# Normalised rows: scaled on the vector engine and transposed, in place of float32 products with a diagonal

## The chip, the core and the metric

The kernel runs on one core of a Trainium2 chip. The metric is device time in microseconds, the median of several runs; the profile is that of one execution.

## The reference

One inference step of a two-layer trunk for 384 tokens (128 context tokens, 256 latent tokens) of width 1024. Each layer has a mixer (retention, Hyena convolution and mLSTM side by side) and a ConvFFN. Ahead of either stands a normalisation with modulation, cut here to what matters:

```python
def rmsnorm(x, g):
    xf = x.astype(jnp.float32)
    return xf * lax.rsqrt(jnp.mean(xf * xf, axis=-1, keepdims=True) + EPS) * g

def trunk_layer(x, cvec, lp, init, latent):
    ...
    h = rmsnorm(x, lp['norm_mix_pre']) * (1.0 + sc1) + sh1
    mix, states = mixer(h, lp, init, latent)
    x1 = x + g1 * rmsnorm(mix, lp['norm_mix_post'])
    h = rmsnorm(x1, lp['norm_ffn_pre']) * (1.0 + sc2) + sh2
    out = x1 + g2 * rmsnorm(conv_ffn(h, lp), lp['norm_ffn_post'])
```

So h is needed four times: for the mixer and for the ConvFFN of two layers.

## The kernel before, in words

**Tiles.** The 384 tokens are three blocks t = 0, 1, 2 of 128 rows; block 0 is the context. `x[t]` holds a block with tokens on partitions and 1024 columns. The projections need h the other way round, with 128 channels on partitions and tokens along the row, in eight pieces, and each piece as a high and a low part in the type fp32r (`hh`, `hl`): every large product is made of three (high by high, high by low, low by high). Weights stream in by DMA (`raw`) and are split in the same way: the scalar engine casts the high part (`hi`), the vector engine subtracts it for the low part (`lo`). In the turns some of these pieces lie in a tile named `aside`.

**From x to h.** `norm_pre(t)` (L732) takes the mean square of a block on the scalar engine, in two halves of 512 columns (`junk`); `rms` (L286) adds them on the vector engine (`rs`) and takes the power -1/2 on GpSimd (`rr`, one value for each row). The vector engine then multiplies an identity matrix by these values, row by row: a diagonal `diag` of 128x128 (L740). `norm_P(t, c)` (L748) multiplies four pieces of 128 columns of x by this diagonal on the tensor engine, in float32; with x as the stationary operand this scales the rows and transposes them in one step, into half c of the block in a PSUM bank. `norm_M` (L756) applies scale and shift of the modulation, four 128x128 pieces for each half (`hf`): half 0 on the scalar engine, half 1 on the vector engine, but for block 1 of the second layer's mixer, where both are on the scalar engine. `norm_S` (L769) casts the high part on the scalar engine (`hh`) and subtracts it on the vector engine (`hl`).

**The four places.** (1) The start, before the mixer of the first layer: `norm_pre` for all three blocks beside the filter spectra, `norm_P` for blocks 0 and 1 ahead of the bias and the last two modulation products (`times(6)`, `times(7)`, L436), `norm_P` for block 2 after the modulation is finished (`start`, L416 to L538). (2) and (4), the turn from mixer to ConvFFN in each layer: `w_out` (L1355) finishes the accumulators of a block, `residual` (L1332) squares them on the scalar engine, multiplies them by the gate on the vector engine (`yg`), takes `rs` and `rr` and adds the result to `x`; then `norm_pre(t)`. The transposition of block 0 is queued between the last products of blocks 1 and 2; those of blocks 1 and 2 stand in `first_up` (L1393), around the first products of the ConvFFN. (3) The turn from the first layer to the second: the same behind the last products of the ConvFFN (L1467 to L1477), with blocks 1 and 2 within the first projection of the mixer (`group`, L784, the branch for `"m"` and group 0).

**Order.** The order on the engines' queues is made by a planner that takes, of the instructions that it believes ready, the one of highest priority; `high_priority(offset=300)` puts residuals and norms ahead of the splits of weights. `issue_after` puts an instruction behind a named one of its engine: `norm_T_after` (L776) puts the products with the diagonal behind all that the tensor engine has been given so far. In the start, `self.strict` fixes the order as written, for the tensor engine first and for vector and scalar engine later.

**Buffers.** `diag` has three buffers in the pool `tmp`, which is opened for the start and again at each turn from mixer to ConvFFN, on the space of the closed mixer pool; the pool of the ConvFFN is opened behind it.

Lines in the traces: L208 is `mm`, L212 is `tp`, L255 `tt`, L260 and L262 `ts`, L266 `stt`, L274 `act`, L278 `copy`.

Of the kernel before, what the change touches and what calls it, by code (L numbers as in the profile page):

```python
# [37 lines left out]
# the largest float32 by which half a turn stays within the range of the sine  # L38
# [3 lines left out]
# ---------------------------------------------------------------- host side: layout and shape constants  # L42
# [8 lines left out]
def _constants():  # L51
# [6 lines left out]
    # minus one for each of the three parts of a head's row  # L58
# [10 lines left out]
    # even and odd tokens, the lower half of the frequencies: the upper half is their sum with  # L69
    # the other sign, conjugated  # L70
# [31 lines left out]
def _layout(inp):  # L102
# [8 lines left out]
    # rows of the modulation vectors: block j of 512 columns sits at partitions 32j (context) and 32j + 1 (latent)  # L111
# [14 lines left out]
    def token_major(m):  # L126
        # (L, D, 4*384) -> per group of 384 columns, two chunks of four 128-row blocks
        m = m.reshape(L, 2, 4, 128, 4, 384)
        return m.transpose(0, 4, 1, 3, 2, 5).reshape(L, 8, 128, 1536)
# [3 lines left out]
    # the gates ride along with the first 384 columns  # L133
# [7 lines left out]
    # per-partition columns  # L141
# [11 lines left out]
    # the filter networks of both layers side by side, 64 partitions each  # L153
# [34 lines left out]
# ---------------------------------------------------------------- device side  # L188

class Trunk:  # L190
    # banks of the accumulators of w_out, by block of tokens
# [13 lines left out]
    # -------- small helpers  # L205
# [8 lines left out]
    def in_order(self, engine):  # L214
        """The engines in self.strict take their work as it is written here."""
        last = getattr(self, engine)
        return self.tc.issue_after(last.ins) if engine in self.strict and last else nullcontext()

    def after(self, *last):
        """Behind these on their engines."""  # L220
        stack = ExitStack()
        for i in last:
            stack.enter_context(self.tc.issue_after(i.ins))
        return stack

    # -------- PSUM: eight banks, each a queue of its own
# [3 lines left out]
    def turn(self, s):  # L230
        """The next bank of a set taken in turns."""
        i = self.turns[s]
        self.turns[s] = i + 1
        return self.bank(self.sets[s][i % len(self.sets[s])])
# [51 lines left out]
    def rms(self, s2):  # L286
        """The reciprocal root of the mean square, from the two halves of the mean."""
        t = self.tiny.tile([128, 1], F32, tag="rs1", name=self.nm("rs"), bufs=4)
        self.stt(t, s2[:, 0:1], EPS, s2[:, 1:2], ALU.add, ALU.add)
        r = self.tiny.tile([128, 1], F32, tag="rr", name=self.nm("rr"), bufs=4)  # L290
        self.nc.gpsimd.tensor_tensor(r, t, self.mhalf[:, 0:1], ALU.pow)  # L291
        return r

    def log_sigmoid(self, out, z, P, n):
        """min(z, 0) - log1p(exp(-|z|)), log1p with the rounding of its argument put back."""
        tl = lambda: self.tiny.tile([P, n], F32, tag=f"ls{n}", name=self.nm("ls"), bufs=4)
        a, e, u, l = tl(), tl(), tl(), tl()
        self.ts(a, z, -1.0, ALU.mult)
        self.tt(a, a, z, ALU.min)
        self.act(e, a, AF.Exp)  # L300
        self.ts(u, e, 1.0, ALU.add)
        self.act(l, u, AF.Ln)
        self.stt(u, u, 1.0, e, ALU.subtract, ALU.subtract)
        self.tt(l, l, u, ALU.subtract)
        self.stt(out, z, 0.0, l, ALU.min, ALU.subtract)

    # -------- weights
# [18 lines left out]
    def load_weights(self):  # L326
        """The loads of the next chunk of the stream, in halves."""
# [14 lines left out]
    def splits(self, key, raws):  # L342
        """High and low parts of a chunk, in steps."""
        halves, steps = [], []
        # at the turn of a block the buffers are still taken, but the one of the spectra is idle
# [5 lines left out]
        for raw in raws:  # L351
            m = raw.shape[1]
            hi, lo = new("hi"), new("lo")
            # finer where the vector engine also has the norms between two projections to do
# [22 lines left out]
    # -------- setup  # L377
    def setup(self):
# [21 lines left out]
        # silu of both conditioning vectors, as stationary columns  # L400
# [15 lines left out]
    def start(self, fp):  # L416
        """Modulation and normalised rows of the first projection, and the filter spectra of both
        layers beside them; the loads in the order in which they are needed."""
# [7 lines left out]
        def rows(k):  # L426
            """Modulation weights, in the buffers of the weights as long as these are idle."""
# [44 lines left out]
        def warm(n):  # L472
            """Products of no use that take the tensor engine's clock out of its rest while the first
            loads are on their way."""
# [18 lines left out]
        # the bias  # L493
# [69 lines left out]
    def fill(self, n=1):  # L563
        """Streams the next blocks of modulation weights beside the projections."""
# [11 lines left out]
    def mod(self, l, s):  # L576
        """Superblock s of the modulation of layer l: (sh1 | sc1), (g1 | sh2), (sc2 | g2)."""
# [11 lines left out]
    def mod_beside(self, l, s):  # L589
        """The same with the products on the vector engine, where only that one has time to spare."""  # L590
# [54 lines left out]
    def gate_rows(self, l, g):  # L645
        """A gate times its norm gain, over all partitions: [128, context / latent, D]."""
# [5 lines left out]
    # -------- hyena filter spectra  # L652
    def filter_hidden(self, fp, w1, w2, col, meanwhile):
        """The hidden layers of the filter networks of both layers: [128, tokens] for each layer,
        64 rows of its own and a row of ones."""
# [4 lines left out]
        for i, wt in enumerate((w1, w2)):  # L660
# [5 lines left out]
            # in turns, less the nearest whole number  # L666
# [15 lines left out]
    def filter_taps(self, fp, l, h, w3):  # L682
        """Sum and difference of the forward and the backward filters."""
# [15 lines left out]
    def filter_spectra(self, fp, l, taps):  # L699
        nc = self.nc  # L700
        # spectra [frequency, tile, cos / sin, order, channel]
# [15 lines left out]
    def butterfly(self, s, d, a, b):  # L717
        """s = a + b, d = a - b, of two PSUM tiles."""
# [8 lines left out]
    # -------- normalised, modulated activations, transposed and split  # L727
# [4 lines left out]
    def norm_pre(self, t):  # L732
        """A diagonal of the reciprocal root mean squares of the rows of x."""
# [5 lines left out]
        d = self.tmp.tile([128, 128], F32, tag="diag", name=self.nm("diag"), bufs=3)  # L739
        self.ts(d, self.ident, r, ALU.mult)  # L740
        self.xn[t] = d

    def norm_T(self, t, where, h, psf):
        """Tokens of block t modulated, transposed and split into the tiles of h."""
# [3 lines left out]
    def norm_P(self, t, c, ps):  # L748
        for k in range(4):
            self.mm(ps[:, 128 * k:128 * k + 128], self.x[t][:, 512 * c + 128 * k:512 * c + 128 * k + 128], self.xn[t])  # L750
        return ps
# [24 lines left out]
    def norm_T_after(self, *a):  # L776
        """norm_T behind the products queued so far."""
# [6 lines left out]
    def group(self, key, l, g, between=None):  # L784
        """Token-major columns g of an input projection: three [128, 384] accumulators."""
# [12 lines left out]
        if key == "m" and g == 0:  # L798
            # the first tokens are there before the last ones
# [36 lines left out]
    def heads_T(self, src, tag):  # L836
        """[128 tokens, 4 * 96] -> [96, 4, 128]."""
# [7 lines left out]
    def head_norm(self, src, out):  # L845
        """out = src * 0.5 * rsqrt(mean(src^2) + eps) by head, [128, 4, 96]; src in SBUF."""
# [9 lines left out]
    # -------- gates of the mLSTM  # L856
    def gates(self, l, pss):
# [5 lines left out]
        # [token, direction, tile, head]  # L863
# [6 lines left out]
        # the splits of the next weights let the gates go first  # L870
# [3 lines left out]
    def stabilisers(self, l, g5, lf):  # L874
# [9 lines left out]
        # rows [head, direction, tile, token]  # L884
# [13 lines left out]
        # [head, (previous, last), direction, tile]  # L898
# [21 lines left out]
        # previous and last stabilisers over all partitions: [128, 2, direction, tile, head]  # L920
# [22 lines left out]
    def row_parts(self, mr):  # L943
        """The stabilisers as three bfloat16 parts that add up to them, 32 partitions apart."""
# [13 lines left out]
    # -------- mLSTM  # L958
# [117 lines left out]
    def channel_major(self, outs, ws, hh, hl):  # L1076
        """Two [128 columns, 384 tokens] products from a chunk [rows of k, 2 * 128 columns]."""
# [9 lines left out]
    # -------- Hyena  # L1087
    def long_conv(self, z, o):
        """z: two [128 channels, 384] tiles -> PSUM tiles of the long convolution, the latent rows
        with the even ones first."""  # L1090
# [10 lines left out]
        # spectra: [frequency, cos / sin, channel] of the context, of the latent rows in two halves  # L1101
# [34 lines left out]
    def conv3(self, out, ps, col):  # L1136
        """Three taps along the tokens, context and latent apart; ps [128, 384] in PSUM."""
# [5 lines left out]
    def hyena(self, l, hs):  # L1143
# [30 lines left out]
        # projections beside the long convolutions  # L1174
# [9 lines left out]
    # -------- retention  # L1184
# [46 lines left out]
    def retention(self, l, M, kd, qd, cd):  # L1231
# [75 lines left out]
        # the first rows of w_out while the gates are on their way  # L1307
# [13 lines left out]
    def token_major(self, outs, blocks, first=False, last=False):  # L1321
        """outs: two [128 tokens, 512] accumulators; blocks: (x high, x low, 128 rows of weights [128, 1024])."""
# [8 lines left out]
    # -------- residual with post-norm  # L1331
    def residual(self, t, accs, g):  # L1332
        """x[t] += g * rmsnorm(accs); accs: two PSUM tiles of 512 columns."""
# [42 lines left out]
    # -------- ConvFFN  # L1376
    def ffn(self, l, g):
        nc = self.nc
        with self.tc.tile_pool(name=f"ffn{l}", bufs=2, reuse_waits="tile") as fp:
# [13 lines left out]
            def first_up():  # L1393
                """The first two chunks, beside the norms: in the order in which the operands get there."""
# [4 lines left out]
                # the context first, while the last latent rows are still being normalised  # L1399
# [16 lines left out]
                # into what the first start has cleared of the banks  # L1416
# [80 lines left out]
    def run(self):  # L1497
# [11 lines left out]
        for l in range(DEPTH):  # L1509
            xp_s.close()  # L1510
            with tc.tile_pool(name=f"mx{l}", bufs=1, reuse_waits="tile") as self.mx:
# [6 lines left out]
                # not among the gates, where it would cost loads of function tables  # L1518
# [45 lines left out]
```

## Time and profile before

| | |
|---|---|
| three runs | 1355.83, 1358.76, 1360.96 us |
| median | 1358.76 us |
| span of the profiled execution | 1355.0 us |
| tensor engine busy | 1339.3 us (99%) |
| vector engine busy | 890.6 us (66%) |
| scalar engine busy | 568.8 us (42%) |
| GpSimd busy | 35.3 us (3%) |
| DMA | 217.27 MB, mean 160 GB/s |

The page gives the profiled execution no time of its own beside its span. The span runs from the first to the last instruction. Engines are called PE (tensor engine), PEld (its weight loads), DVE (vector engine), ACT (scalar engine), POOL (GpSimd). A row such as `diag<-c_ident,rr` says what is written and, behind the arrow, what is read; `b` is a PSUM bank. A float32 product appears as two instructions, products of fp32r and transposes as one. Products overlap in the tensor engine: the next one starts before the last has ended, so the step from one start to the next is what it costs the engine, and the time shown for a run of products is from the first start to the last end.

### The profile page before, as it was taken

The page shows a single profiled execution, that of the slowest core. Times are in us where ns is not written, and L with a number is a line of the kernel's source. Part 1 is how long each engine was busy: PE and PEld are TensorE (multiplying, and loading weights), DVE is VectorE, ACT ScalarE, POOL GpSimd, SP SyncE. Part 2 cuts the span into 40 slices and gives each one's busy share as a digit, 9 for nine tenths or more (in the row PEclk, how much of TensorE's full clock was granted, in tenths as well). Part 3 has the DMA queues.
Part 4 walks back from the last instruction along what each step waited for, and adds up shares of the span by engine and source line. Part 5 has one row for each costly group of instructions (what it writes and reads, how often), then busy time and mean ns, then how long its engine had stood idle before and what let it go on. Part 6 is the DMA issues. An engine that isn't in the chain of part 4 may idle for free.

```text
span 1355.0 us, 19419 instructions
## 1 busy us (share of the span) xinstructions
PE 1339.3 (99%) x7527; PEld 1206.1 (89%) x7527; DVE 890.6 (66%) x1594; ACT 568.8 (42%) x944; POOL 35.3 (3%) x64
## 2 busy tenths in 40 slices
PE   8999999999999999999999999999999999999997
PEld 2788788889998998899899999988999999999996
DVE  5657666667887899799557578666645545545445
ACT  3654253464333333333247543546433333333333
POOL 1100000000000000000000000000000000000000
PEclk9999999999999999999999999999999999999999
DMA  9864557344665565665335232424434334333331
GB/s 354 290 249 148 181 168 238 101 164 151 212 227 172 191 237 176 212 221 181 116 112 192 95 95 73 143 92 173 143 118 137 126 117 136 124 121 131 124 122 50
DMA packets 59101, 217.27 MB, mean 160 GB/s; under 512 B 7214, under 2 KB 9456, under 8 KB 53632
## 3 DMA queue, kind: packets, MB, share of 16 engines
q1 hardware_dynamic: 59008, 216.02, 46.7%
q8 instruction: 59, 0.97, 0.3%
q14 instruction: 34, 0.28, 0.1%
HBM read 210.06 MB, written 5.94 MB: 159 GB/s over the span
## 4 chain that ended last, share of the span: by engine, by line
PE 91%; DMA 5%; DVE 2%; ACT 1%; issue 1%; POOL 0%; SPq 0%; DVEq 0%; POOLq 0%; ACTq 0%
PE b L208 90%; DMA mraw<-in_w_mod 1%; DMA raw<-in_w_up 1%; PE b L212 1%; DMA hi<-in_w_mod 1%; DMA lo<-in_w_mod 1%; DMA raw<-in_w_in_m 1%; DVE lo L255 1%; ACT junk L274 0%; ACT hi L278 0%; DMA c_tri<-in_c_tri 0%; DMA w<-in_f_w 0%; DVE mr L908 0%; POOL rr L291 0%; DVE x L266 0%
## 5 line engine op out<-in xcount | busy, mean ns | idle before, releaser
L255 DVE TENSOR_TENSOR lo<-raw,hi 128x1024 fp32r<-128x1024 f32 (+3 forms) x288 | 321.2, 1129 | 216.9 <-ACT hi L278 214.3
L278 ACT CAST hi<-raw 128x1024 fp32r<-128x1024 f32 (+3 forms) x288 | 275.4, 973 | 411.7 <-PE b L208 387.5
L208 PE MATMUL b<-hh,lo 128*128 128x384 f32 (+1 forms) x1120 | 367.9, 336 | 0.0
L208 PE MATMUL b<-hh,hi 128*128 128x384 f32 (+2 forms) x1120 | 364.8, 334 | 0.0
L208 PE MATMUL b<-hl,hi 128*128 128x384 f32 x1088 | 362.5, 338 | 0.0
L208 PEld LDWEIGHTS b<-hh,hi 128*128 128x128 f32 x1120 | 205.7, 188 | 4.6 <-issue 2.5
L208 PEld LDWEIGHTS b<-hh,lo 128*128 128x128 f32 x1120 | 208.0, 188 | 0.1
L208 PEld LDWEIGHTS b<-hl,hi 128*128 128x128 f32 x1088 | 203.7, 188 | 1.2
L208 PE MATMUL b<-lo,hh 128*128 128x384 f32 (+2 forms) x474 | 164.8, 352 | 1.9 <-DVE lo L255 1.9
L208 PE MATMUL b<-hi,hh 128*128 128x384 f32 (+2 forms) x468 | 165.5, 357 | 0.9 <-ACT hh L1347 0.8
L208 PE MATMUL b<-hi,hl 128*128 128x384 f32 (+2 forms) x468 | 162.7, 351 | 0.0
L266 DVE SCALAR_TENSOR_TENSOR cv<-b,pcol,cv 128x127 f32<-128x127 f32 (+1 forms) x256 | 100.6, 414 | 93.9 <-ACT cv L274 89.4
L208 PE MATMUL b<-lo,gh 128*128 128x512 f32 x384 | 151.7, 395 | 0.0
L208 PE MATMUL b<-hi,gh 128*128 128x512 f32 x384 | 150.6, 392 | 0.0
L208 PE MATMUL b<-hi,gl 128*128 128x512 f32 x384 | 150.2, 391 | 0.0
L274 ACT ACTIVATE cv<-b,pcol 128x384 f32<-128x384 f32 x64 | 43.0, 672 | 178.6 <-PE b L208 178.4
L266 DVE SCALAR_TENSOR_TENSOR macc<-mraw,sil,macc 128x512 f32<-128x512 f32 x168 | 113.3, 746 | 0.0
L208 PEld LDWEIGHTS b<-hi,hh 128*128 128x128 f32 x468 | 87.8, 188 | 16.1 <-issue 8.0
L208 PEld LDWEIGHTS b<-lo,hh 128*128 128x128 f32 x474 | 89.1, 188 | 7.3 <-DVE lo L255 3.7
L208 PEld LDWEIGHTS b<-hi,hl 128*128 128x128 f32 x468 | 87.9, 188 | 4.5 <-issue 0.7
L208 PEld LDWEIGHTS b<-hi,gh 128*128 128x128 f32 x384 | 72.1, 188 | 17.5 <-issue 2.5
L208 PEld LDWEIGHTS b<-lo,gh 128*128 128x128 f32 x384 | 72.1, 188 | 17.2 <-issue 3.4
(242 smaller groups left out, 1221.2 us busy)
## 6 DMA issues: line engine op xcount, KB each, us to landing
raw<-in_w_up SPq DMA_DIRECT2D x128, 512.0 KB, 4.6
mraw<-in_w_mod SPq DMA_DIRECT2D x40, 1024.0 KB, 5.1
raw<-in_w_down SPq DMA_DIRECT2D x64, 512.0 KB, 4.3
raw<-in_w_in_r SPq DMA_DIRECT2D x32, 384.0 KB, 3.1
raw<-in_w_in_m SPq DMA_DIRECT2D x24, 384.0 KB, 6.3
raw<-in_w_out SPq DMA_DIRECT2D x16, 512.0 KB, 4.1
raw<-in_w_in_h SPq DMA_DIRECT2D x12, 512.0 KB, 3.7
mraw<-in_w_mod SPq DMA_DIRECT2D x8, 512.0 KB, 10.0
```

The source lines that it names most:

```text
L208: self.pe = self.nc.tensor.matmul(out, lhsT=lhsT, rhs=rhs, start=start, stop=stop, **kw)
L212: self.pe = self.nc.tensor.transpose(out, in_, self.ident[:n, :n])
L255: self.dve = self.nc.vector.tensor_tensor(o, a, b, op)
L266: self.dve = self.nc.vector.scalar_tensor_tensor(o, a, s, b, op0, op1)
L274: self.scalar = self.nc.scalar.activation(o, a, f, **kw)
L278: self.scalar = self.nc.scalar.copy(o, a)
```

## The change

`norm_pre` no longer makes a diagonal. It multiplies the two halves of x by the reciprocal root mean square on the vector engine, into two tiles `xs` of 128x512 float32, six buffers in the same pool. `norm_P` transposes four pieces of such a half by `tp`, the transpose of the tensor engine with the identity, in place of the products of x with the diagonal. Everything else is as before; comments that went are left out here.

```diff
     def norm_pre(self, t):
-        """A diagonal of the reciprocal root mean squares of the rows of x."""
         s2 = self.tiny.tile([128, 2], F32, tag="s2", name=self.nm("s2"), bufs=6)
         for c in range(2):
             jk = self.tmp.tile([128, 512], BF16, tag="junkn", name=self.nm("junk"), bufs=1)
             self.act(jk, self.x[t][:, 512 * c:512 * c + 512], AF.Square, scale=D ** -0.5, accum_out=s2[:, c:c + 1])
         r = self.rms(s2)
-        d = self.tmp.tile([128, 128], F32, tag="diag", name=self.nm("diag"), bufs=3)
-        self.ts(d, self.ident, r, ALU.mult)
-        self.xn[t] = d
+        halves = []
+        for c in range(2):
+            xs = self.tmp.tile([128, 512], F32, tag="xs", name=self.nm("xs"), bufs=6)
+            self.ts(xs, self.x[t][:, 512 * c:512 * c + 512], r, ALU.mult)
+            halves.append(xs)
+        self.xn[t] = halves
...
     def norm_P(self, t, c, ps):
         for k in range(4):
-            self.mm(ps[:, 128 * k:128 * k + 128], self.x[t][:, 512 * c + 128 * k:512 * c + 128 * k + 128], self.xn[t])
+            self.tp(ps[:, 128 * k:128 * k + 128], self.xn[t][c][:, 128 * k:128 * k + 128])
         return ps
```

## Rows read from the trace of the kernel before

**Rows 1.** The page's table of engines: busy time, share of the span, instructions

```profile
PE 1339.3 (99%) x7527; PEld 1206.1 (89%) x7527; DVE 890.6 (66%) x1594; ACT 568.8 (42%) x944; POOL 35.3 (3%) x64
```

**Rows 2.** The chain that ended last, in order of time: start, us, what

```profile
284.78 0.30 DVE diag L260
285.13 155.55 PE b L208 x890
...
708.63 23.93 PE b L208 x140
```

**Rows 3.** Timeline of PE, first turn from mixer to ConvFFN: start, us, instruction

```profile
285.13 2.05 PE L208 MATMUL b<-diag,x 128*128 128x128 f32 x16 [0.16 <-DVE diag L260]
...
292.52 1.95 PE L208 MATMUL b<-diag,x 128*128 128x128 f32 x16
...
298.27 0.61 PE L208 MATMUL b<-hh,lo 128*128 128x128 f32 x4
...
299.61 2.00 PE L208 MATMUL b<-diag,x 128*128 128x128 f32 x16
...
303.18 2.60 PE L208 MATMUL b<-hh,aside 128*128 128x256 f32 x20
```

**Rows 4.** DVE timeline; window: busy PE, PEld, DVE, ACT, POOL, granted clock, DMA

```profile
284.99 1.43 DVE L255 TENSOR_TENSOR yg<-b,G 128x512 f32<-128x512 f32 x2
...
291.22 1.28 DVE L255 TENSOR_TENSOR lo<-raw,aside 128x512 fp32r<-128x512 f32 x2
...
298.93 0.29 DVE L260 TENSOR_SCALAR diag<-c_ident,rr 128x128 f32<-128x128 f32 x1 [0.41 <-POOL rr L291]
...
284.80:299.90 15.10, 14.94 (x108) 13.78 (x108) 12.86 (x29) 12.05 (x30) 2.20 (x4) 1.00 0.27 102
```

**Rows 5.** The same turn: timeline of ACT

```profile
300.75 1.51 ACT L274 ACTIVATE hf<-b,modT,modT 128x128 f32<-128x128 f32 x4 [1.58 <-PE b L208]
302.29 1.37 ACT L278 CAST hh<-hf 128x512 fp32r<-128x512 f32 x2
```

**Rows 6.** Groups by line and form: count | busy us, mean ns | idle before

```profile
L208 PE MATMUL b<-diag,x 128*128 128x128 f32 x192 | 23.8, 278 | 1.1 <-DVE diag L260 1.0 <-ACT hf L274 0.2
...
L260 DVE TENSOR_SCALAR macc<-mraw,sil 128x512 f32<-128x512 f32 x24 | 9.8, 480 | 1.7 <-DMA mraw<-in_w_mod 1.7
...
L212 PE MATMUL b<-c_ident,hs 128*128 128x128 f32 x36 | 5.0, 275 | 0.0
```

**Rows 7.** Timeline of PE in the first mixer: twelve transposes, a product behind them

```profile
82.33 1.47 PE L212 MATMUL b<-c_ident,k 128*96 128x128 f32 x12
...
85.18 0.33 PE L208 MATMUL b<-hi,hl 128*128 128x384 f32 x1
```

**Rows 8.** Timeline of DVE: four scalings of 128x512 in a row

```profile
336.17 1.67 DVE L260 TENSOR_SCALAR macc<-mraw,sil 128x512 f32<-128x512 f32 x4
```

**Rows 9.** Timeline of the start: PE, DVE, ACT

```profile
34.57 3.84 PE L208 MATMUL b<-diag,x 128*128 128x128 f32 x32 [0.35 <-DVE diag L260]
...
44.73 2.05 PE L208 MATMUL b<-diag,x 128*128 128x128 f32 x16 [0.17 <-ACT hf L274]
...
41.20 0.88 DVE L266 SCALAR_TENSOR_TENSOR modbm<-b,c_onecol,modbm 128x256 f32<-128x256 f32 x2 [5.08 <-PE b L208]
...
39.20 1.99 ACT L278 CAST hi<-raw 128x400 fp32r<-128x400 f32 x4 [9.37 <-DMA raw<-in_w_in_q]
```

**Rows 10.** Timeline of DVE and PE in the turn from layer to layer

```profile
721.02 1.05 DVE L255 TENSOR_TENSOR lo<-raw,hi 128x400 fp32r<-128x400 f32 x2
...
721.08 1.50 PE L208 MATMUL b<-lo,hh 128*128 128x400 f32 x6
...
724.23 1.25 PE L208 MATMUL b<-lo,hh 128*128 128x400 f32 x6
```

**Rows 11.** Timeline of PE in the start: float32 products

```profile
4.51 1.65 PE L208 MATMUL b<-feat,w 33*128 33x384 f32 x2
...
26.48 4.56 PE L208 MATMUL b<-w,fh 128*128 128x512 f32 x10
```

## The prediction

> **What bounds the kernel now.** I read the engine table first. The tensor engine is busy for 99% of the span and the vector engine for 66% [rows 1], so over the whole kernel the change trades time of the engine that is full for time of one that is not. That is only an average, so I read next the chain of work in order of time. It shows the four places where rows are normalised: the start, the turn from mixer to ConvFFN in either layer, and the turn from the first layer to the second. At the last three the chain leaves the vector engine's `diag` and stays with the tensor engine from there on: 890 instructions in a row from 285.13, 140 from 708.63 [rows 2] (the turn of the second layer, at 930.22, repeats the first). So no wait ends late behind a diagonal today, and every product with one lies on the path. The timelines of such a turn are the third view. The tensor engine does the diagonal products of block 0 at 285.13, of block 1 at 292.52 and of block 2 at 299.61, with other products packed between [rows 3]. Block 2 is the tight one. Its `diag` is finished at 299.22 [rows 4], the scalar engine waits 1.58 us for the first half of its products and ends the first half of `hh` at about 302.9 (302.29 + half of 1.37) [rows 5], and the first products that need this start at 303.18 [rows 3]. The slack is about 0.25 us.
>
> **The tensor engine's part.** The change takes away eight float32 products of x with a diagonal per block and puts eight transposes there. The trace records 192 instructions for the 96 products, so two for each [rows 6]. What counts is how long the engine starts them: the run of 16 less the last one's own 0.27 us, which is 2.05 - 0.27 = 1.78 us for block 0 and 1.95 - 0.27 = 1.68 for block 1 [rows 3]. Twelve transposes of the same 128 columns take 1.47 us with the last one's own 0.27 in it, which is (1.47 - 0.27) / 11 = 0.109 us each [rows 6, 7]. Eight make 0.87 us. A block is thus 0.91 or 0.81 us shorter, a turn of three blocks 2.5 us.
>
> The Trainium skill (TensorE: Matmul & The Clock Gate, Part 4) has about 275 ns for a transpose within a kernel. Eight of these one after another would be 2.2 us, and a block would get longer by some 0.4 us, the kernel by some 5 us. The trace has the same duration, 275 ns [rows 6], but starts them 0.109 us apart [rows 7], so I use the spacing.
>
> **The vector engine's part.** It loses one 128x128 scaling of 0.29 us per block [rows 4] and gets two of 128x512. The nearest row of this form (scalar from a column, float32, SBUF to SBUF) is the first step of `macc`: 480 ns for one [rows 6], 1.67 us for four in a row, so 0.40 us from start to start [rows 8]. A pair holds the queue for 0.8 us where the diagonal held it for 0.2 (284.78 to 284.99 [rows 2, 4]): 0.6 us more per block, 7 us in all. The first transpose can start 0.48 - 0.29 = 0.2 us later than the first product did. The second half is there 0.40 us after the first, and four transposes take 0.44, so no second wait comes of it. Nothing is added to the GpSimd or DMA queues.
>
> What stands behind the pair is `yg` of the next block, which has to run before that block's root mean square, residual and second norm. So the pair of block 0 delays the route of block 1, and that of block 1 the route of block 2. From 284.8 to 299.9 the vector engine is busy for 12.86 of 15.10 us [rows 4]; what is left are mostly waits for GpSimd's power, which lie on the route itself. The one filler ahead of block 2's `yg` is a weight split of 1.28 us at 291.22 [rows 4], which no product uses before 298.27 [rows 3].
>
> **Turns from mixer to ConvFFN.** I follow the route to the products at 303.18. Good end: the accumulators of block 2 are ready 0.91 - 0.2 = 0.7 us earlier; the scaling is 0.2 us later; the first four transposes save 0.46; and the 0.39 us for which the finished `diag` waited for the tensor engine (299.22 to 299.61) goes. Together -1.4 us, not the 2.3 that the tensor engine alone would give (2.5 less the 0.2 of the first wait), since the scalar engine's route is late next. Bad end: both pairs push the route by 1.2 us in all and the earlier accumulators help nothing: 1.2 + 0.2 - 0.46 - 0.39 = +0.55, less the slack of 0.25, +0.3. The planner may put the split behind `yg`, which takes back about one of the two pairs. I take -0.5 for each of the two turns.
>
> **Turn from layer to layer.** Here the vector engine's splits bind already. The last two `lo` pieces end at 722.07, and the six products of block 0 that use them take 1.50 us where the same six of block 1 take 1.25 [rows 10]. What the first two blocks save ends at these pieces. Ends: +1.2 us (both pairs ahead of the pieces) and -1.4 us (the pairs lie in gaps and the good end of the other turns holds). They are about as far apart on either side, and the late pieces speak for the upper half, so I take 0.
>
> **The start.** The 32 instructions for blocks 0 and 1 take 3.84 - 0.27 = 3.57 us; 16 transposes take 1.75, from 0.2 us later: -1.6 us. The vector engine waits 5.08 us for the tensor engine behind this, up to 41.20, so six scalings (2.5 us) find room. The modulation products between would end at 39.6 and need their last loads about a microsecond before; the load queued behind these had landed by 39.20, when the scalar engine's wait for it ended [rows 9]. Block 2's products at 44.73 (2.05 - 0.27 = 1.78) become 0.87, of which 0.2 may go to a wait for `hl`: -0.7. Sum -2.3; ends -2.5, and -0.7 if the loads come too late for the first part.
>
> **The buffers.** `diag` takes 3 x 512 bytes a partition, `xs` 6 x 2 KB. Tiles behind it in the same pool and the ConvFFN's pool move up by 10.5 KB onto other tiles of the closed mixer pool. By the code these are written only behind the residuals of `w_out`, when all of the mixer's tiles have been read, so I count nothing. If that cover fails, a tile waits for its predecessor's last reader; the one wait of this size that a turn has room for is the slack of 0.25 us.
>
> **The sum.** -2.3 - 0.5 - 0.5 + 0 = -3.3 us. The profiled span is 1355.0, 0.8 below the fastest of the three runs (1355.83) and 3.8 below their median. The page has no other time of that execution, so I take the difference off the median: 1358.8 - 3.3 = 1355.5.
>
> **Rivals.** *The whole saving is kept.* Three turns at 2.3 and a start of 2.5 us: -9.4 us, 1349.4. For it speaks that the tensor engine is on the chain throughout [rows 2]; against it the slack of 0.25 us at block 2 and the late `lo` pieces. 0.2.
>
> *The vector queue becomes the bound, and the kernel gets slower.* The place is block 2 of each turn: its scaled rows come late, and the tensor engine stands at the transposes. It decides from the point where the route of block 2 is over 0.25 us later than today. Price: the bad ends (+0.3, +0.3, +1.2) and once in each turn a filler of 1.28 us that the planner puts into the gap of the route [rows 4], +3.8; with the start's -2.3 this is +3.3, 1362.1. For it speaks that the vector engine is nearly full there, against it that such fillers have lower priority. 0.2.
>
> *The clock falls.* The first two float32 products of the kernel take 1.65 us with 384 columns each, ten with 512 columns at 26 us take 4.56 [rows 11]: 0.83 against 0.46 us a product, so half the speed does occur, while in the turn the granted clock is 1.00, the level of 2.4 GHz [rows 4]. If transposes brought it back for the 5.6 us of products between blocks 0 and 1 (285.13 + 1.78 to 292.52 [rows 3]) in each turn, this would add 17 us to the forecast of the first rival: 1366. The Trainium skill (TensorE: Matmul & The Clock Gate, Part 4) says that the fast clock does not engage in transposes. The trace speaks against a fall: after twelve of them in a row the products of 384 columns still take 0.33 us [rows 7]. 0.04.
>
> **How the numbers follow.** My forecast of a saving partly given back has 0.56 and by itself reaches from 1352 to 1360; its sum has ends at -2.5 - 3 x 1.4 = -6.7 and at -0.7 + 0.3 + 0.3 + 1.2 = +1.1. With the two large rivals the range is 1349.0 to 1362.5; the clock and the outer half of the second rival lie outside. About 0.5% (6.8 us) is what can be told from no change. Faster by more: most of the first rival and the edge of the forecast, 0.18. Slower by more: the clock and the tail of the second rival, 0.1. The rest, 0.72, is within.
>
> **What would show it.** Right: blocks at 0.87 us on the tensor engine; pairs of 0.88 us on the vector engine; the products now at 303.18 only some half a microsecond closer to 285.13; a wait for `xs` before the transposes of block 2. The first rival is right if that wait is missing and the turn is 2.3 us shorter; the second if it passes 2 us. Wrong would be transposes spaced much wider than 0.11 us, scalings over 0.6 us, or an order of the queues that differs beyond the turns.

## The result, and the profile after

The change makes the kernel slower. The median after is 1366.63 us (5 runs, 1364.82 to 1368.14) against 1358.76 us for the 5 runs of the kernel before that were made beside them: a ratio of 1.0055, 95% interval 1.0041 to 1.007, or 7.5 us (5.6 to 9.5). The forecast was 1355.5, and the range ended at 1362.5.

The page of the kernel after, where it answers to [rows 1]: its span, and the engines' busy time, share and instructions.

```profile
span 1364.9 us, 19231 instructions
...
PE 1341.2 (98%) x7431; PEld 1206.2 (88%) x7431; DVE 897.0 (66%) x1606; ACT 568.1 (42%) x944; POOL 34.9 (3%) x64
```

The tensor engine has 96 instructions less and is busy for 1.9 us longer. A kernel that does less on an engine and keeps it busy for longer has run it more slowly somewhere, and the turn from mixer to ConvFFN shows where. First the tensor engine's timeline of that turn (start, us, instruction, in brackets the idle time ahead of it and what ended it), which answers to [rows 3]:

```profile
282.74 1.09 PE L212 MATMUL b<-c_ident,xs 128*128 128x128 f32 x8 [0.36 <-DVE xs L260]
...
289.18 1.04 PE L212 MATMUL b<-c_ident,xs 128*128 128x128 f32 x8
...
294.02 0.39 PE L208 MATMUL b<-hh,lo 128*128 128x128 f32 x2
297.62 0.69 PE L208 MATMUL b<-hh,lo 128*128 128x128 f32 x2 [3.21 <-DVE lo L255]
...
299.82 1.93 PE L212 MATMUL b<-c_ident,xs 128*128 128x128 f32 x8
...
304.85 3.92 PE L208 MATMUL b<-hh,aside 128*128 128x256 f32 x20
308.61 0.64 PE L208 MATMUL b<-hh,lo 128*128 128x256 f32 x4
```

Three things are to be read here. The transposes of a block take 1.09 and 1.04 us where the products with the diagonal took 2.05 and 1.95, as forecast. Between the two halves of four products that stood together at 298.27 before [rows 3], the engine now waits 3.21 us, and what it waits for is `lo`, a low part of the weights, and not `xs`. And behind that wait everything lasts longer: the same eight transposes take 1.93 us, and the twenty products of 256 columns 3.92 us for 2.60 before. The busy times by stretch of that turn give the reason. The columns are PE, PEld, DVE, ACT, POOL, each with its count, then the granted clock of the tensor engine, the DMA share and GB/s:

```profile
290.00:294.40 4.40, 4.40 (x41) 4.27 (x38) 4.00 (x8) 3.77 (x11) 0.55 (x1) 1.00 0.31 97
294.40:297.60 3.20, 0.01 (x1) 0.00 (x0) 2.76 (x8) 1.04 (x3) 0.55 (x1) 1.00 0.50 195
297.60:301.40 3.80, 3.78 (x19) 3.78 (x19) 0.69 (x1) 0.49 (x3) 0.00 (x0) 0.50 0.39 138
301.40:305.00 3.60, 3.60 (x19) 3.60 (x18) 3.18 (x7) 2.27 (x5) 0.00 (x0) 0.50 0.00 0
305.00:307.00 2.00, 2.00 (x11) 2.00 (x11) 1.94 (x4) 0.00 (x0) 0.00 (x0) 0.50 0.08 18
307.00:309.00 2.00, 2.00 (x16) 2.00 (x15) 0.00 (x0) 0.00 (x0) 0.00 (x0) 0.80 0.80 260
309.00:320.00 11.00, 11.00 (x78) 11.00 (x77) 5.86 (x11) 6.58 (x9) 0.00 (x0) 1.00 0.42 142
```

The engine stands for 3.2 us, and from then on the granted clock is 0.50, the level of 1.2 GHz, for some 10 us, before it is back at 1.00 (2.4 GHz). In the kernel before it was 1.00 up to 299.9 [rows 4], and it reads 1.00 from there to 310 too. In the page's row of the clock the whole fall of this turn is a single 8 among forty digits, since a slice there is 34 us.

The vector engine's timeline of the turn, which answers to [rows 4], shows why the low part is late:

```profile
288.51 0.88 DVE L260 TENSOR_SCALAR xs<-x,rr 128x512 f32<-128x512 f32 x2 [0.34 <-POOL rr L291]
289.30 0.68 DVE L255 TENSOR_TENSOR lo<-raw,aside 128x512 fp32r<-128x512 f32 x1
289.91 0.68 DVE L255 TENSOR_TENSOR hl<-hf,hh 128x512 fp32r<-128x512 f32 x1
290.51 1.28 DVE L255 TENSOR_TENSOR yg<-b,G 128x512 f32<-128x512 f32 x2
...
295.77 0.88 DVE L260 TENSOR_SCALAR xs<-x,rr 128x512 f32<-128x512 f32 x2 [0.41 <-POOL rr L291]
296.56 0.40 DVE L262 TENSOR_SCALAR hf<-b,modT,modT 128x128 f32<-128x128 f32 x1
296.89 0.68 DVE L255 TENSOR_TENSOR lo<-raw,aside 128x512 fp32r<-128x512 f32 x1
```

Before, the two pieces of this split stood together at 291.22. The planner has now put only one of them there and the other 7.6 us later (289.30 to 296.89), behind the whole route of block 2 with its scaled rows. The turn of the second layer is the same: a wait of 3.20 us that ends at 949.81, the clock at 0.50 behind it. In the list of waits the tensor engine's time for `lo` goes from 1.9 to 9.4 us.

The other two places. At the start, transposes stand where [rows 9] had the products:

```profile
35.60 1.99 PE L212 MATMUL b<-c_ident,xs 128*128 128x128 f32 x16 [0.55 <-DVE xs L260]
...
43.90 1.09 PE L212 MATMUL b<-c_ident,xs 128*128 128x128 f32 x8 [0.16 <-ACT hf L274]
```

The block 0 scaling of the first turn starts at 282.20, 2.58 us earlier than before (284.78 [rows 2]). Across the turn from layer to layer the distance to the kernel before hardly changes.

To compare the kernels without what came earlier in each, I take the length of a turn from two rows: for the two turns from mixer to ConvFFN, from the start of block 0's scaling (`diag` or `xs`) to the twenty products of 256 columns; for the turn from layer to layer, from the same scaling to the first product of 128x384 behind it. In us, from the profiled execution of each kernel:

| kernel | first turn | layer to layer | second layer's turn | granted clock behind the `lo` products |
|---|---|---|---|---|
| before | 18.40 | 24.84 | 18.41 | 1.00 |
| after | 22.65 | 24.64 | 22.64 | 0.50 |
| 1: low parts first | 18.02 | 24.68 | 18.03 | 1.00 |
| 2: filler products | 19.46 | 24.66 | 19.47 | 1.00 |
| 3: scaled rows alone | 18.71 | 26.02 | 18.72 | 1.00 |
| 4: transposes alone | 16.50 | 23.29 | 16.49 | 1.00 |
| 9: before, last low part late | 21.46 | 24.79 | 23.08 | falls to 0.50 |
| 10: before, both late | 23.63 | 24.82 | 24.19 | falls to 0.50 |

The slow clock reaches beyond the point at which this measure ends: the twenty products themselves take 1.3 us more (3.92 against 2.60). Up to the `lo` products behind them the first turn of the kernel after is 5.6 us longer than before, not 4.25.

### The profile page after: what moved, and what is told of

Its sections match the earlier page's. It is cut to its first block, busy times and chain, and to the rows that moved or that the text cites. A ratio compares the mean times of both kernels' runs of the same rounds, so it can differ in the third digit from the quotient of the medians.

```text
span 1364.9 us, 19231 instructions
## 1 busy us (share of the span) xinstructions
PE 1341.2 (98%) x7431; PEld 1206.2 (88%) x7431; DVE 897.0 (66%) x1606; ACT 568.1 (42%) x944; POOL 34.9 (3%) x64
## 4 chain that ended last, share of the span: by engine, by line
PE 88%; DVE 4%; DMA 4%; ACT 1%; issue 1%; POOL 1%; SPq 0%; POOLq 0%; DVEq 0%; ACTq 0%
PE b L208 87%; PE b L212 2%; DMA raw<-in_w_up 1%; DMA mraw<-in_w_mod 1%; DVE x L266 1%; DVE lo L255 1%; POOL rr L291 1%; DMA x<-in_xs 1%; DMA hi<-in_w_mod 1%; DMA raw<-in_w_in_m 1%; DVE yg L255 1%; DVE xs L260 0%; ACT junk L274 0%; DVE hl L255 0%; ACT hi L278 0%
## 5 line engine op out<-in xcount | busy, mean ns | idle before, releaser
L208 PEld LDWEIGHTS b<-hh,hi 128*128 128x128 f32 x1120 | 209.0, 192 | 4.6 <-issue 2.5
```

Of the source, the lines that this page charges most:

```text
L208: self.pe = self.nc.tensor.matmul(out, lhsT=lhsT, rhs=rhs, start=start, stop=stop, **kw)
```

## The experiments

My theory after the result: the low part of a weight split was put behind block 2's scaled rows, the tensor engine waits for it, and the idle time costs it the clock. Rival 1: the scaled rows fill the vector queue, and the wait would only move to another tile. Rival 2: the transposes cost the clock. All ratios below are to the kernel before, run beside.

### Experiments 1 and 8: the low parts first

```diff
-                    lambda h=h, l=l, r=r: self.tt(l, r, h.bitcast(F32), ALU.subtract)))
+                    lambda h=h, l=l, r=r: self.low(key, l, r, h)))
...
+    def low(self, key, l, r, h):
+        with self.tc.high_priority(offset=300) if key in (("u", 0, 0), ("u", 1, 0)) else nullcontext():
+            self.tt(l, r, h.bitcast(F32), ALU.subtract)
```

> The changed kernel, with the low parts of the first two weight splits of each ConvFFN (lo<-raw,aside) given a higher priority, so that they come ahead of the scaled rows of block 2 on the vector engine; the tensor engine's order stays. Theory (the tensor engine waits 3.2 us for the second low part, and the idle time then costs it the clock for some 10 us): no wait above 1 us for a low part in the two turns from mixer to ConvFFN, the granted clock stays at 1.00 there, each turn 7 to 8 us shorter than in the changed kernel, time 1349 to 1355. Rival 1 (the scaled rows themselves fill the vector queue): the wait moves to the transposes of block 2, over 2 us of idle time stay in each turn, time 1358 to 1364. Rival 2 (the transposes cost the clock): the idle time goes, but the clock still falls to 0.50 behind them, about 3 us shorter per turn, time 1358 to 1361.

Measured: 1353.75 us, ratio 0.9977 (0.9967 to 0.9987), 3.1 us under the kernel before; so the place of two vector instructions in each of the two turns is worth the whole 7.5 us loss and 3.1 us more. The vector engine's timeline of the first turn has the pair together again, ahead of the scaled rows of block 1:

```profile
286.00 1.28 DVE L255 TENSOR_TENSOR lo<-raw,aside 128x512 fp32r<-128x512 f32 x2
...
288.62 0.88 DVE L260 TENSOR_SCALAR xs<-x,rr 128x512 f32<-128x512 f32 x2 [0.34 <-POOL rr L291]
...
295.92 0.88 DVE L260 TENSOR_SCALAR xs<-x,rr 128x512 f32<-128x512 f32 x2 [0.41 <-POOL rr L291]
```

On the tensor engine the waits that are left come in pieces:

```profile
296.46 1.09 PE L212 MATMUL b<-c_ident,xs 128*128 128x128 f32 x8 [0.49 <-DVE xs L260]
...
299.88 2.66 PE L208 MATMUL b<-hh,aside 128*128 128x256 f32 x20 [0.59 <-ACT hh L278]
```

and the granted clock stays:

```profile
294.00:298.00 4.00, 3.51 (x32) 3.37 (x32) 2.91 (x9) 1.81 (x6) 0.55 (x1) 1.00 0.41 158
298.00:302.00 4.00, 3.41 (x29) 3.27 (x29) 3.80 (x9) 2.42 (x6) 0.00 (x0) 1.00 0.01 4
302.00:306.00 4.00, 4.00 (x36) 4.00 (x35) 2.98 (x7) 2.00 (x3) 0.00 (x0) 1.00 0.50 150
```

Against rival 1: the wait did move to `xs` and then to `hh`, but with 0.49 and 0.59 us, and the turn is 0.38 us shorter than before, not longer. My 7 to 8 us for a turn was too much: up to the `lo` products behind the twenty it is 5.9 us shorter than in the kernel after (20.51 against 26.41). The same kernel once more, beside experiments 5 to 7:

> The first experiment once more, beside the two versions that are compared with it: the same ratio to the kernel before, 0.9967 to 0.9987.

Measured: 1354.19 us, ratio 0.9977 (0.9964 to 0.9989), turns of 18.03, 24.67 and 18.03 us.

### Experiment 2: the wait kept, the idle time filled

```diff
                 for n, c, k in steps:
+                    if warm and (n, c, k) == (2, 0, 6):
+                        with self.after(self.pe):
+                            spin = self.bank(self.WO[2][0]).rearrange("p (h n) -> p h n", h=4)
+                            for _ in range(14):
+                                self.mm(spin, self.ident_b, self.negmask[:, 0:1, :].to_broadcast([128, 4, 128]))
...
-                up_part(a, w, (0, 128), ((hh, 0), (hl, 0), (hh, 1)), product(range(3), range(2), range(KD)))
+                up_part(a, w, (0, 128), ((hh, 0), (hl, 0), (hh, 1)), product(range(3), range(2), range(KD)), warm=True)
```

> The changed kernel, with 14 bf16 products of 128x512 into an unused bank put behind the sixth step of the third pass in each up projection's first token group, so that the tensor engine has work where it waits for the low part. Theory: the vector engine's order and the end of the wait stay (the next product with lo starts about when it did), but with the idle time filled the granted clock stays at 1.00 and each turn is some 4 to 5 us shorter: 1356 to 1360. Rival 2 (the transposes cost the clock): the clock falls to 0.50 as before, and the fillers add up to 3 us per turn: 1366 to 1373.

Measured: 1357.44 us, ratio 1.0005 (0.9993 to 1.0018), some 6.8 us less than the change alone by the two ratios (7.5 - 0.7). The tensor engine's timeline of the first turn:

```profile
293.36 3.19 PE L208 MATMUL b<-negmask,identb 128*128 128x512 bf16 x14
296.73 0.44 PE L208 MATMUL b<-hh,lo 128*128 128x128 f32 x2 [0.17 <-DVE lo L255]
...
297.90 1.06 PE L212 MATMUL b<-c_ident,xs 128*128 128x128 f32 x8
...
300.77 2.66 PE L208 MATMUL b<-hh,aside 128*128 128x256 f32 x20
```

The products with the late `lo` start 15.42 us after the turn's scaling (281.31), as in the kernel after (297.62 - 282.20 = 15.42), so the wait is untouched. But the transposes behind it take 1.06 us and not 1.93, and the clock is 1.00 throughout:

```profile
293.00:297.00 4.00, 3.83 (x21) 1.92 (x21) 3.51 (x10) 1.55 (x5) 0.55 (x1) 1.00 0.52 185
297.00:301.00 4.00, 3.93 (x36) 3.79 (x36) 2.07 (x6) 2.40 (x6) 0.00 (x0) 1.00 0.42 131
```

This splits the loss of a turn. From experiment 1 to experiment 2 the turn grows by 1.44 us (18.02 to 19.46): that is what the late low part costs as a wait. It is less than the 3.2 us of the wait itself for two reasons: in experiment 1 the engine comes to the low parts 0.8 us later in the turn (12.61 us behind the scaling, for 11.83), and the smaller waits of experiment 1 (0.49 and 0.59 us in the rows above) are gone behind the late low part. From experiment 2 to the kernel after it grows by 3.19 us, and by 1.3 more in the twenty products: about 4.5 us are the clock's. Fourteen products of no use are thus a gain.

### Experiments 6, 9 and 10: the late low part alone, in the kernel before

If the theory holds, the kernel before must get slower from the place of this one split, with no scaled row and no transpose in it. The first try hung the piece behind the last diagonal emitted when the split is written, which is not yet that of block 2, so the vector engine's order stayed as it was:

```diff
...
+        with self.after(self.scaled) if last and key in (("u", 0, 0), ("u", 1, 0)) else nullcontext():
+            self.tt(l, r, h.bitcast(F32), ALU.subtract)
```

> The kernel before with one thing moved: the last low part of the first weights of each ConvFFN is put behind the diagonal of block 2 on the vector engine, where the changed kernel has it behind the scaled rows. No product and no scaling changes. Theory (the place of this low part is what cost the changed kernel its time): the tensor engine, which comes to it at about 298.6 in the kernel before, waits 1 to 2 us in each of the two turns; if that wait takes the clock too, 4 to 6 us more per turn; in all 2 to 12 us slower than the kernel before, and the wait for lo is in the list of waits. Rival (the split is harmless, the scaled rows or the transposes are the cause): within 1 us of the kernel before, no such wait.

Measured: 1356.58 us, ratio 1.0001 (0.999 to 1.0012), with both pieces still together at 289.89. It tells nothing of the theory. Experiments 9 and 10 write the piece, or both, behind the norm of block 2:

```diff
-                    lambda h=h, l=l, r=r: self.tt(l, r, h.bitcast(F32), ALU.subtract)))
+                    lambda h=h, l=l, r=r, last=raw is raws[-1] and a + g == m: self.low(key, l, r, h, last)))
...
         self.xn[t] = d
+        self.scaled = self.dve
...
                 self.norm_pre(t)
+        while self.late:
+            self.late.pop(0)()
...
+        if last and key in (("u", 0, 0), ("u", 1, 0)):
+            with_after = lambda: self.behind(f)
+            self.late.append(with_after)
...
```

(Experiment 10 has `last=raw is raws[-1]`; `behind` issues the piece after `self.scaled`.)

> The kernel before, with the last low part of the first weights of each ConvFFN written behind the norm of block 2 and held behind its diagonal on the vector engine (what the sixth experiment meant to do). The tensor engine's order stays, and no product and no scaling changes. Theory (the place of this low part is what cost the changed kernel its time): the tensor engine comes to it at about 298.4 in the kernel before and gets it at 299.8 to 300.3, so it waits 1.4 to 1.9 us in each of the two turns, 2.8 to 3.8 us slower in all; if the clock falls behind these waits too, up to 12 us slower. Rival (the split is harmless, the scaled rows or the transposes are the cause): within 1 us of the kernel before.

> The same with both low parts of that half behind the diagonal of block 2. Theory: the tensor engine waits for the first one too, 1.6 to 2.5 us from 298.3 on in each turn, in all 3.5 to 6 us slower than the kernel before without a fall of the clock, 8 to 16 us slower with one. Rival: within 1 us of the kernel before.

Measured: experiment 9 1363.43 us, ratio 1.0063 (1.0045 to 1.0082), 8.5 us slower; experiment 10 1368.66 us, ratio 1.0096 (1.0076 to 1.0116), 13.0 us slower. The tensor engine's timeline of experiment 9, first turn:

```profile
297.43 0.38 PE L208 MATMUL b<-hh,lo 128*128 128x128 f32 x2
299.03 0.44 PE L208 MATMUL b<-hh,lo 128*128 128x128 f32 x2 [1.22 <-DVE lo L255]
...
300.38 3.45 PE L208 MATMUL b<-diag,x 128*128 128x128 f32 x16
```

and its busy times by stretch:

```profile
294.00:299.00 5.00, 3.81 (x35) 3.67 (x33) 4.28 (x11) 3.02 (x7) 0.83 (x2) 1.00 0.65 210
299.00:300.40 1.40, 1.37 (x11) 1.37 (x11) 0.57 (x1) 0.00 (x0) 0.00 (x0) 0.85 0.16 32
300.40:303.80 3.40, 3.40 (x19) 3.40 (x19) 0.00 (x0) 1.37 (x4) 0.00 (x0) 0.56 0.41 146
303.80:305.40 1.60, 1.60 (x17) 1.60 (x16) 1.53 (x5) 0.90 (x3) 0.00 (x0) 1.00 0.00 0
```

A wait of 1.22 us is enough here: the products with the diagonal behind it take 3.45 us in place of 2.00 [rows 3], and the two turns grow by 3.1 and 4.7 us, 7.7 of the 8.5. The place of one vector instruction of 0.68 us costs the old kernel about what the whole change cost. In experiment 10 the engine waits 1.44 and 0.51 us for the two pieces of the first turn, and the products behind the first wait already run at 0.50. No transpose of rows ran in either kernel, so the fall of the clock does not need one; experiment 4 below shows the other half, that transposes alone do not bring it.

### Experiments 3 and 4: each half of the change alone

Experiment 3 scales the rows and turns them with float32 products; experiment 4 turns the rows by transposes, without the scaling.

```diff
 e3, from the kernel after:
-            self.tp(ps[:, 128 * k:128 * k + 128], self.xn[t][c][:, 128 * k:128 * k + 128])
+            self.mm(ps[:, 128 * k:128 * k + 128], self.xn[t][c][:, 128 * k:128 * k + 128], self.ident)
 e4, from the kernel before:
-            self.mm(ps[:, 128 * k:128 * k + 128], self.x[t][:, 512 * c + 128 * k:512 * c + 128 * k + 128], self.xn[t])
+            self.tp(ps[:, 128 * k:128 * k + 128], self.x[t][:, 512 * c + 128 * k:512 * c + 128 * k + 128])
```

> The vector part of the change alone: rows are scaled on the vector engine, and then turned by float32 products with the identity in place of transposes. Theory: the low part is still put behind the scaled rows of block 2, and the tensor engine, which comes to it about 1.7 us later per turn, waits 1.5 to 3.3 us for it; where it does, the clock falls though no transpose ran: 1361 to 1372. Rival 2: without transposes the clock stays at 1.00 in the turns, and the time is 1357 to 1361. Rival 1 (the scaled rows fill the vector queue): over 2 us of waits for xs in each turn.

> The tensor part of the change alone: the kernel before with transposes of the rows as they are, in place of the products with the diagonal; the scaling is left out (the diagonal is still made, but nothing reads it). Theory: without the scaled rows on the vector queue both low parts come early, the tensor engine keeps 0.8 us per block, the clock stays at 1.00: 1346 to 1352. Rival 2: the clock falls to 0.50 behind the transposes in the turns, 1355 to 1365.

Measured: experiment 3 1357.11 us, ratio 1.0008 (0.9995 to 1.002); experiment 4 1349.91 us, ratio 0.9945 (0.9927 to 0.9963). So the halves alone are worth +1.1 us, which can't be told from nothing, and -7.5 us, and both together +7.5: nearly 14 us come from their meeting. For experiment 3 my theory missed, as I had taken its order to be that of the kernel after. The vector engine's timeline shows the pair together:

```profile
290.63 1.28 DVE L255 TENSOR_TENSOR lo<-raw,aside 128x512 fp32r<-128x512 f32 x2
...
297.70 0.88 DVE L260 TENSOR_SCALAR xs<-x,rr 128x512 f32<-128x512 f32 x2 [0.40 <-POOL rr L291]
```

The tensor engine comes to these low parts at 296.84 and waits for nothing. Its time falls into the numbers of rival 2, but not for that rival's reason, since experiment 4 has all the transposes and keeps the clock in the turns. The tensor engine's timeline of experiment 4 around block 2, and its busy times by stretch:

```profile
296.08 1.06 PE L212 MATMUL b<-c_ident,x 128*128 128x128 f32 x8
...
299.99 2.66 PE L208 MATMUL b<-hh,aside 128*128 128x256 f32 x20 [1.11 <-ACT hh L278]
```

```profile
295.00:299.00 4.00, 3.88 (x36) 3.74 (x34) 2.79 (x8) 2.43 (x7) 0.55 (x1) 1.00 0.61 250
299.00:303.00 4.00, 3.01 (x25) 3.01 (x26) 3.91 (x9) 1.53 (x3) 0.00 (x0) 1.00 0.02 4
303.00:307.00 4.00, 4.00 (x36) 4.00 (x35) 2.97 (x7) 2.86 (x4) 0.00 (x0) 1.00 0.74 235
```

Eight transposes of 1.06 us run at 296.08 here, and the granted clock is 1.00 before, in and behind them; in experiment 9 it falls without any. The Trainium skill (TensorE: Matmul & The Clock Gate, Part 4) says that the fast clock does not engage in transposes. The measurement differs and decides: these eight take 1.06 us at 1.00, the same eight behind the wait of the kernel after take 1.93 us at 0.50, and no fall in the turns goes with transposes.

Why the planner splits the pair only when both halves are there was not tried and stays open.

### Experiments 5 and 7: the start alone, and the best version

Experiment 5 calls `norm_pre(t, True)` in the start alone, and makes the diagonal and its products elsewhere:

```diff
-            self.norm_pre(t)
+            self.norm_pre(t, True)
...
+        if not scaled:
+            d = self.tmp.tile([128, 512], F32, tag="xs", name=self.nm("diag"), bufs=6)[:, :128]
+            self.ts(d, self.ident, r, ALU.mult)
+            self.xn[t] = d
+            return
...
```

> The change in the start alone: scaled rows and transposes for the first projection, the diagonal and its products in all four later turns. It prices the term of the start, which the prediction put at 2.3 us of gain (2.5 to 0.7). Theory: the gain is there in full and nothing later gives it back, 1.5 to 2.5 us under the kernel before (ratio 0.9982 to 0.9989). Rival (the start ends on loads and the gain is lost there): within 0.5 us of the kernel before.

Measured: 1355.02 us, ratio 0.9983 (0.9971 to 0.9995), -2.3 us (-3.9 to -0.7). Its three turns last 18.51, 24.83 and 18.50 us, as before within 0.1. Experiment 7 adds the keys of the turn from layer to layer to experiment 1:

```diff
-        with self.tc.high_priority(offset=300) if key in (("u", 0, 0), ("u", 1, 0)) else nullcontext():
+        with self.tc.high_priority(offset=300) if key in (("u", 0, 0), ("u", 1, 0), ("m", 1, 0), ("m", 1, 1)) else nullcontext():
```

> The changed kernel with the low parts moved up as in the first experiment, and those of the first two weights of the layer-to-layer turn too. Theory: the waits for lo in the third turn (1.0 and 0.2 us in the changed kernel) go, and the time is 0 to 2 us under the first experiment's, 1351.5 to 1354. Rival: the moved low parts push the scaled rows of that turn back, and the time is the first experiment's or up to 2 us above it.

Measured: 1353.52 us, ratio 0.9973 (0.9962 to 0.9984). One wait of 0.57 us for `lo` is left in the turn from layer to layer, which is 23.76 us, 0.9 shorter than in experiment 8 (24.67), but the medians are 0.7 us apart with ranges that overlap, so the two can't be told apart by time. Either beats both kernels: by its ratio some 3 to 4 us under the one before, which itself is 7.5 under the changed one.

## Why the prediction was wrong

- **The tensor engine's part held.** Eight transposes take 1.09 and 1.04 us with the last one's own time; by starts 0.85 and 0.79 for the predicted 0.87 (282.74 to 283.59, 289.18 to 289.97).
- **The vector engine's part held.** A pair takes 0.88 us and holds the queue for 0.79 (288.51 to 289.30).
- **The start held.** Predicted -2.3; experiment 5 measures -2.3 (-3.9 to -0.7).
- **The turn from layer to layer held.** Predicted 0, between +1.2 and -1.4; its length changes by -0.2. Experiment 3 has nearly the upper end (+1.18) and experiment 4, which has no scaled rows, goes past the lower one (-1.55).
- **The turns from mixer to ConvFFN are the step that failed.** I took -0.5 each, between -1.4 and +0.3; they grew by 5.6 and 5.5 us (the first from 20.84 to 26.41 us up to the `lo` products behind the twenty). The words that failed are those on the weight split: a filler "which no product uses before 298.27", of which the planner's deferral "takes back about one of the two pairs". It did defer one piece, as I thought, but I entered this as a gain and never asked how late it might go. In the kernel before the split ends at 292.50, 5.8 us ahead of its products. Counted from the turn's scaling, the engine now comes to them 1.7 us earlier (11.82 us, for 298.27 - 284.78 = 13.49), and the second piece ends at 15.37 (297.57 - 282.20) where it ended at 7.72: a slack of some 6 us has become a wait of 3.21.
- **The clock was priced for the wrong cause.** I had a rival in which it falls, but for transposes. Here it falls behind idle time of the tensor engine, and about 4.5 of the 5.6 us of a turn are its share (experiment 2). The rows that I took for half speed [rows 11] count instructions, two to a float32 product, so they are one product of 384 columns and five of 512, and the granted clock reads 1.00 over both stretches: they leave open what made the difference.
- **With the low parts in place the forecast was right.** In experiment 1 the turns are 0.38 us shorter for the predicted 0.5, and the whole is 3.1 us (1.8 to 4.5) under the kernel before for the predicted 3.3. The route is the one I followed: the engine waits 0.49 us for `xs` ahead of block 2's transposes and then for the scalar engine's `hh`. That the number is met so closely is partly luck, since -0.5 was a choice between ends of -1.4 and +0.3, and the slack in it was 0.20 and not 0.25 us (302.29 + half of 1.37 is 302.98, against 303.18). Experiment 1 keeps the six buffers of `xs` and loses nothing that would point to them, so my 0 for the buffers held as far as can be seen. The rival of the slower vector queue named block 2's scaled rows as the place and a filler of 1.28 us as part of its price; a filler did decide, but what became late was half of the filler itself, and not the scaled rows.

The sum for the kernel after: -2.3 for the start, +5.6 and +5.5 for the two turns, -0.2 for the third, is +8.6 us. The median says +7.5 (5.6 to 9.5), the spans of the two profiled executions +9.9; of what the sum lacks there, 1.2 us lie between the turn from layer to layer and the second layer's turn (197.95 against 196.74 us from the first 128x384 product to the scaling).

## What to carry to other kernels

Where a planner orders a queue by priority, a low-priority item has a due time of its own: work it out from the first instruction that reads it, take off what the change saves ahead of that instruction, and ask what happens if the item goes behind the whole new work. Price a new wait on a saturated tensor engine at the wait and, as a second case, at the slower clock that may follow it; in the kernel after the second was three times the first. And test a change of two halves with each alone and with the old order of the other queues put back: the change here was a gain of 3 us under a loss of 11 that it only set off.

## What the runs showed of the hardware that was not expected

The fall of the clock hangs on more than the length of one wait. It fell to 0.50 behind waits of 3.21 us (the kernel after) and 1.22 us (experiment 9), but experiment 4 has a longer wait than the second of these, in the turn from layer to layer, and the granted clock reads 1.00 in and behind it, from 714 to 728 us:

```profile
718.56 0.45 PE L208 MATMUL b<-lo,hh 128*128 128x400 f32 x1 [1.26 <-DVE lo L255]
```

Nor does the fall come at a fixed point of the wait. In the first turn of the kernel after, the granted clock still reads 1.00 during the 3.2 us of idle time, and 0.50 from the next instruction on. In experiment 9 it stays at 1.00 for some 0.9 us behind the wait, and reads 0.50 from 300 to 303. The way back differs too: in the first turn of experiment 9 the clock was back at 1.00 by 303.80, some 5 us behind the wait, in the kernel after only some 10 us behind it.

There is a second place of this kind, in the gates behind the turn from layer to layer. In experiment 5, whose turns are those of the kernel before, the granted clock is 0.63 from 750 to 754 us; in the kernel before it is 1.00 there, and in the kernel after 0.69. Of the twelve profiled executions eight show a fall between 742 and 762 us, experiments 1, 7 and 8 among them, and the kernel before and experiments 2, 4 and 6 do not. Each is one profiled execution, and what decides there was not tried.
